# Gates and branches of a decoder's mixer by rows of tokens, the gates' first 512 columns as one seven-product unit, part of the weight splitting on GpSimd

## The chip, the core and the metric

The kernel runs on one core of a Trainium2 chip. The metric is the device time of one launch in microseconds. Before the change it is 1186.37 us, the median of three runs (1186.35 to 1187.4). The engines are called by their names in the profile: PE (TensorE, matmuls), PEld (its weight loads), DVE (VectorE), ACT (ScalarE), POOL (GpSimd), SP (SyncE, which issues most DMAs). Each of them works through its own queue in order.

## What is computed

A decoder trunk of two layers on 256 tokens of width 1024, all in float32. A layer is a feed-forward half step, a mixer, and another feed-forward half step. The change is in the mixer, which is this (shortened):

```python
z = x @ w_in
u, v, q, k, val, gates = jnp.split(z, SPLITS, axis=-1)
h_a = _chunked_sgu(gelu(u), gelu(v), sgu_ln_g, sgu_ln_b, sgu_w, sgu_b)
o = _diff_attention(_rope(q), _rope(k), val, lam_full)       # 8 heads, causal
h_b = _rmsnorm(o, diff_ln_g) * (1.0 - lam_init)
g = jax.nn.sigmoid(gates.reshape(bsz, seq, N_BRANCH, D_MODEL) + gate_b)
m = g[:, :, 0] * (h_a @ w_branch[0]) + g[:, :, 1] * (h_b @ w_branch[1])
return m @ w_out
```

Each of the seven parts of `w_in` (u, v, q, k, val, gate A, gate B), each branch matrix and `w_out` is 1024 x 1024.

## The kernel before

**Exactness.** A float32 product is made of three fast matmuls. Every operand is split into a high part (ScalarE copies it into the rounded format) and a low part (VectorE subtracts the high part from the value): hi and lo. A product is hi x hi, lo x hi and hi x lo. `split` (L245), `stream` (L176) and `pieces` (L362) do this.

**Weights** come in chunks of 128 x 2048 words (1 MB), loaded by SyncE into one of `RAW` = 4 buffers (`fetch`, L159). A chunk is two half chunks of 128 x 1024; for each, ScalarE writes a hi and VectorE a lo buffer, of which there are `HL` = 8 each. So weights are prepared up to four chunks ahead, and then the preparing engines wait until TensorE has given buffers back.

**Two forms of a projection.** By rows (`gemm_b`, L324, with `rows_b`, L314): 128 tokens of x are the stationary operand, 512 columns of weights stream by, the result stands tokens by columns. One step (128 of the inner dimension, 128 tokens) is three matmuls of 512 (L283). By columns (`gemm_a2`, L285): 128 columns of weights are stationary, and the hi and lo of x, 2 x 256 tokens, stream by as one matmul of 512 (L295), and for the lo weights hi of x alone, a matmul of 256 (L302). The result stands columns by tokens; it lies in two halves of a PSUM bank, so ScalarE copies one out (L303) and VectorE adds the other (L305).

**Seven products.** The feed-forward layers do part of their products by Strassen's scheme: 2 x 2 blocks (two blocks of 128 tokens by two of 512 inner dimensions, times two by two blocks of weights) take seven block products instead of eight. VectorE adds the blocks of x (`strassen_sums`, L860) and of weights (`plus`, L356), or a DMA on GpSimd's queue adds one weight block to another in its buffer (`gather`, L350). `product` (L372) is one of them: 12 matmuls of 512 (L376). They are taken one at a time between chunks of other work.

**Order.** TensorE's order is the program's. Work of the other engines that goes on beside it is written as generators with delays (`beside`, L137, `beat`, L124), counted in units of matmul work; two chunk halves by rows for both token blocks are two units. The order on the other engines is made by the scheduling layer from these priorities.

**The mixer (L969).** val by rows; then for each of four head pairs q and k by columns with rotary (`rope`, L984: the swapped copy goes by DMA, GpSimd multiplies it, L993), and `attend` (L1003) beside it: scores on TensorE (L1017), mask and maximum on VectorE (L1029), exponentials on ScalarE (L1031), differences on VectorE (L1040), a transpose by DMA that needs the 16-bit words of each number apart and joined again (`parted` by GpSimd L216, `joined` by ScalarE L1065), the product with val (L1071, L1073), then the root of the sum of squares as a chain of small operations on GpSimd (`rsqrt4`, L265 to L277), which ScalarE's scaling (L1090) waits for, and another transpose. The two gates follow, for each the first 512 columns by rows (`gate_rows`, L1119) and the second 512 by columns (`gate_columns`, L1130). Then u, v, spatial gating, and the branches: `branch_rows` (L1211) and `branch_columns` (L1243). The merged m is needed columns by tokens for the output projection; the half by rows is transposed (`turned`, L1222: L216 and L1227 part the words, SyncE's DMA transposes, L229 joins them), the half by columns is split at once. The output projection (`gemm_b2`, L467) takes m's first half of columns first for the first 128 tokens, and the second half first for the second.

Of the kernel before, what the change touches and what calls it, by code (L numbers as in the profile page):

```python
# [45 lines left out]
RAW, HL = 4, 8  # L46
RSQRT_START = -554050368.0

# [6 lines left out]
def trunk(ctx, tc, x, xT, w13a, w13b, w2, wb, wqk, wu, wg, wgr, wbr, wbrr, wo, gateb, gatebr, sgug, sgub, sguwT, sgubias, lam, diffg,  # L55
# [42 lines left out]
    def t512(s, n=3):  # L98
        return tmp.tile([P, 512], F32, tag="main", name=name(s), bufs=n)

    def s512(s, n=4):
        return tmp.tile([P, 512], F32, tag="side", name=name(s), bufs=n)
# [45 lines left out]
    line = [None, None, False]  # L148

# [26 lines left out]
    def stream(src, width=CH, sub=HC, lent=(), after=(None, None), pool=()):  # L176
# [3 lines left out]
        raw = fetch(src, width)  # L180
        out = []
# [174 lines left out]
    def plus(raw, more):  # L356
        for v, m in zip(halved(raw), halved(more)):
            with behind(line[1]):
                inline(V, V.tensor_tensor(out=v, in0=v, in1=m, op=ALU.add).ins)  # L359
        return raw  # L360

    def pieces(raw):  # L362
        out = []
        for v in halved(raw):
# [187 lines left out]
    gbh = const.tile([P, DEPTH, 2, KT], F32, name="gbh")  # L552
# [4 lines left out]
    def setup(after):  # L557
# [3 lines left out]
        for dst, src in ((x_tok[0], x[:P, :]), (x_tok[1], x[P:, :]), (cos_t, cosT), (sin_t, sinT), (dgs, diffg),  # L561
                         (gbh, gateb), (ln_g, lngT), (ln_b, lnbT), (lam_t, lam.partition_broadcast(P))):
# [6 lines left out]
        with behind(added[0]):  # L569
            V.tensor_scalar(out=gbh, in0=gbh, scalar1=0.5, scalar2=None, op0=ALU.mult)  # L570
# [23 lines left out]
    class Norm:  # L594
# [36 lines left out]
        def kept(self):  # L631

            y = self.y[-1][:, D - self.group :]
            unit, v = (tmp.tile([P, 512], F32R, tag="main", name=name("kept"), bufs=3) for _ in range(2))
# [145 lines left out]

    def ffn(l, f, i, norm, last=False):
# [57 lines left out]
        def sums_of_h():  # L839
# [3 lines left out]
            made.append([tmp.tile([P, 512], F32R, tag="side", name=name("sum"), bufs=4) for _ in range(2)])  # L843
            yield from strassen_sums(sums, made, h11, h21, h12, h22, 1.5)

        def sums_of_x():
# [6 lines left out]
            def home(tag):  # L853
                pool, n = {"main": (tmp, 3), "side": (tmp, 4), "slot": (act, 26)}[tag]
                return pool.tile([P, 512], F32R, tag=tag, name=name("xhs"), bufs=n)
# [3 lines left out]

        def strassen_sums(to, made, v11, v21, v12, v22, apart=1, after=lambda: None):  # L860
            to[:] = [tuple(lambda k, v=v: v[:, k * P : (k + 1) * P] for v in m) for m in made]
            for n, (out, a, b, op) in ((0, (v22, v21, v22, ALU.subtract)), (2, (v21, v11, v21, ALU.subtract)),
                                       (1, (v11, v22, v11, ALU.subtract)), (3, (v12, v12, v11, ALU.add))):
                with behind(after()):
                    V.tensor_tensor(out=out, in0=a, in1=b, op=op)
                if n in (2, 3):
                    yield apart
            for n, out in ((0, v22), (2, v21), (1, v11), (3, v12)):
                split(*(v if len(out.shape) == 2 else v.rearrange("p (k t) -> p k t", k=4) for v in made[n]), out)
                yield apart  # L870
# [98 lines left out]
    def mixer(l, i, norm):  # L969
        xh, xl = parts(both)  # L970
# [32 lines left out]
        def attend(hp, qT, kT):  # L1003
# [17 lines left out]
            def exps(t, banks):  # L1021
                nk = (t + 1) * P
                pp = []
                for m in range(2):
                    o = m * 4 + t * 2
                    p = s512("pp", 4)[:, : 2 * nk]
# [39 lines left out]
            yield 2 if hp else 1.5  # L1066
# [15 lines left out]
            yield 0.8  # L1082
# [3 lines left out]
            yield 3.6 if hp < 3 else 2.6  # L1086
# [4 lines left out]
            yield 0.4  # L1091
            onT = slots("onT", 2)[0]
            parted(on, onT)
            yield 3.4 if hp < 2 else 1.4
            moved(onT, on)
            yield 1.8
            with behind(added[0]):
                joined(on, onT, V)
            yield 0.3
# [9 lines left out]

        for hp in range(HEADS // 2):  # L1110
# [3 lines left out]
            if hp == 1:  # L1114
                gbias = bc_load(gatebr[l], qT[:, :1])

        gates, grow = [], []

        def gate_rows(br):  # L1119

            gr = [slots("gr", 2)[0] for _ in range(NT)]
            grow.append(gr)

            def done(t, ps, c, n):
                added[0] = V.tensor_tensor(out=gr[t], in0=ps, in1=gbias[:, br * 512 : (br + 1) * 512], op=ALU.add).ins
                emptied[0] = A.activation(gr[t], gr[t], AF.Tanh, scale=0.5).ins

            gemm_b(wgr[l, br, 0], KT, xh, xl, done, tail=TAIL)

        def gate_columns(br):  # L1130
            gt = slots("gate", KT // 2)
            gates.append(gt)
            for c in range(KT // 4):
                (_, b), = gemm_a2([wg[l, br, c]], both, lambda m: t512("gz"), lambda: t512("r"))
                for n in range(2):
                    s, k = slice(n * T, (n + 1) * T), KT // 2 + c * 2 + n
                    A.activation(gt[c][:, s], b[:, s], AF.Tanh, scale=0.5, bias=gbh[:, l, br, k : k + 1])

        for br in range(2):
            gate_rows(br)  # L1140
            gate_columns(br)

        g_bc, b_bc = (bc_load(v[l], gates[0][0][:, :1]) for v in (sgug, sgub))
# [214 lines left out]
```

## Time and profile before

| | us |
|---|---|
| median of three runs | 1186.37 (1186.35 to 1187.4) |
| span of the profiled execution, first to last instruction | 1185.1 |
| what lies around the span, median less span | 1.3 |
| PE busy | 1180.5 |
| DVE busy | 1013.1 |
| ACT busy | 828.1 |
| POOL busy | 287.5 |
| mean granted clock of TensorE | 1.000 |
| HBM read | 248.05 MB, 210 GB/s over the span |

How it is read: the page gives busy time and the chain of waits that ended last; groups give the mean time of an instruction by line and shape; the timeline gives start and length of instructions in order; windows give busy times by stretch. Busy rows of matmuls overlap, so what a matmul costs is read from the start of one to the start of the next. The first mixer stands at about 180 to 420 us, the second at about 770 to 1010.

### The profile page before, as it was taken

The numbers are of one execution on the slowest core, as the hardware profiler recorded it, in microseconds if no ns is written. First come the engines' busy times: TensorE is split into PE (matmuls) and PEld (weight loads), VectorE is DVE, ScalarE is ACT, GpSimd is POOL, SyncE is SP. The second block draws the span as 40 slices with busy tenths as digits, with TensorE's granted clock in tenths as the row PEclk, the third lists the DMA queues.
The fourth block names the chain that finished last, engine by engine and source line by source line (L and its number), as shares of the span: only waits on it lengthen the run. The fifth ranks groups of instructions, "written<-read, shape, count | busy, mean of one in ns | idle before, by whom it ended". The sixth has DMA issues, their size and how long they took to land.

```text
span 1185.1 us, 16676 instructions
## 1 busy us (share of the span) xinstructions
PE 1180.5 (100%) x5777; PEld 995.0 (84%) x5777; DVE 1013.1 (85%) x1562; ACT 828.1 (70%) x1419; POOL 287.5 (24%) x350
## 2 busy tenths in 40 slices
PE   9999999999999999999999999999999999999998
PEld 8888888888888888888888888888888888888887
DVE  6989989788688989889899889888965989988895
ACT  6688658559955677876667876576788556679761
POOL 1011201247420220051020161003564112102600
PEclk9999999999999999999999999999999999999999
DMA  9869976767865658699668689586666755786881
GB/s 355 265 198 262 287 273 208 266 193 238 246 205 173 227 188 273 187 275 267 239 220 265 190 278 280 198 290 232 212 204 208 250 181 174 247 254 208 273 260 36
DMA packets 129621, 275.10 MB, mean 232 GB/s; under 512 B 89041, under 2 KB 90369, under 8 KB 105473
## 3 DMA queue, kind: packets, MB, share of 16 engines
q1 hardware_dynamic: 121968, 248.67, 63.5%
q0 software_dynamic: 6992, 24.71, 8.7%
q8 instruction: 45, 0.74, 0.2%
q10 hardware_dynamic: 576, 0.66, 0.2%
q14 instruction: 40, 0.32, 0.1%
HBM read 248.05 MB, written 1.05 MB: 210 GB/s over the span
## 4 chain that ended last, share of the span: by engine, by line
PE 99%; DVE 0%; DVEq 0%; issue 0%
PE bank L283 46%; PE bank L295 15%; PE sbank L376 12%; PE bank L410 10%; PE bank L302 8%; PE sbank L410 3%; PE bank L530 2%; PE sbank L1017 1%; PE bank L376 1%; PE sbank L1073 1%; PE sbank L1191 1%; PE sbank L542 0%; PE sbank L1071 0%; PE sbank L714 0%; DVE xtok L701 0%; DVE st L643 0%
## 5 line engine op out<-in xcount | busy, mean ns | idle before, releaser
L197 DVE TENSOR_TENSOR wlo<-raw,whi 128x1024 fp32r<-128x1024 f32 (+1 forms) x346 | 379.4, 1123 | 51.8 <-ACT whi L195 38.0
L195 ACT ACTIVATE whi<-raw 128x1024 fp32r<-128x1024 f32 (+1 forms) x350 | 323.4, 952 | 135.1 <-PE bank L283 43.0
L283 PE MATMUL bank<-whi,x 128*128 128x512 f32 x1224 | 386.4, 390 | 0.0
L283 PEld LDWEIGHTS bank<-whi,x 128*128 128x128 f32 x1224 | 229.8, 188 | 47.8
L283 PE MATMUL bank<-wlo,x 128*128 128x512 f32 x612 | 238.2, 389 | 0.0
L249 DVE TENSOR_TENSOR wlo<-raw,whi 128x1024 fp32r<-128x1024 f32 (+1 forms) x123 | 142.9, 1185 | 20.3 <-ACT whi L247 11.4
L247 ACT ACTIVATE whi<-raw 128x1024 fp32r<-128x1024 f32 (+1 forms) x123 | 121.1, 1003 | 51.2 <-DVE raw L359 23.9
L295 PE MATMUL bank<-x,whi 128*128 128x512 f32 x640 | 153.3, 391 | 0.0
L295 PEld LDWEIGHTS bank<-x,whi 128*128 128x128 f32 x640 | 118.2, 188 | 23.8
L283 PEld LDWEIGHTS bank<-wlo,x 128*128 128x128 f32 x612 | 114.9, 188 | 23.1
L229 POOL COPY seven<-seven 128x512 uint16<-128x512 uint16 x16 | 58.8, 3733 | 135.2 <-ACT whi L195 54.6
L302 PEld LDWEIGHTS bank<-x,wlo 128*128 128x128 f32 x640 | 81.4, 191 | 2.9
L302 PE MATMUL bank<-x,wlo 128*128 128x256 f32 x640 | 82.6, 283 | 0.0
L410 PE MATMUL bank<-whi,hhi 128*128 128x512 f32 (+1 forms) x182 | 68.2, 374 | 0.0
L410 PE MATMUL bank<-whi,hlo 128*128 128x512 f32 (+1 forms) x182 | 67.9, 373 | 0.0
L410 PE MATMUL bank<-wlo,hhi 128*128 128x512 f32 (+1 forms) x182 | 67.9, 373 | 0.0
L993 POOL TENSOR_TENSOR swap<-swap,sin_t 128x512 f32<-128x512 f32 x16 | 26.9, 1680 | 101.2 <-DMA swap<-z 84.4
L757 POOL COPY nvia<-ntwo 128x256 uint16<-128x256 uint16 x20 | 10.0, 547 | 161.2 <-DMA ntwo<-nvia 148.2
L303 ACT ACTIVATE r<-bank 128x256 f32<-128x256 f32 x96 | 34.9, 373 | 16.3 <-PE bank L302 16.1
L376 PE MATMUL sbank<-whi,xhs 128*128 128x512 f32 x128 | 42.0, 389 | 0.0
L410 PEld LDWEIGHTS bank<-whi,hlo 128*128 128x128 f32 x182 | 34.3, 188 | 6.0
L410 PEld LDWEIGHTS bank<-whi,hhi 128*128 128x128 f32 x182 | 34.3, 188 | 6.0
(292 smaller groups left out, 2157.6 us busy)
## 6 DMA issues: line engine op xcount, KB each, us to landing
raw<-in_w13b SPq DMA_DIRECT2D x68, 1024.0 KB, 6.0
raw<-in_w SPq DMA_DIRECT2D x32, 1024.0 KB, 7.0
raw<-in_wb SPq DMA_DIRECT2D x16, 1024.0 KB, 6.7
raw<-in_wqk SPq DMA_DIRECT2D x16, 1024.0 KB, 6.2
home<-in_w13b SPq DMA_DIRECT2D x16, 512.0 KB, 5.9
raw<-in_w13a SPq DMA_DIRECT2D x8, 1024.0 KB, 4.9
home<-in_w SPq DMA_DIRECT2D x16, 512.0 KB, 4.9
raw<-in_wgr SPq DMA_DIRECT2D x8, 1024.0 KB, 5.4
```

The lines of the kernel that those rows point to most:

```text
L195: inline(A, A.activation(h, r, AF.Copy).ins)
L197: low = eng.tensor_tensor(out=w, in0=r, in1=h.bitcast(F32), op=ALU.subtract).ins
L229: eng.tensor_copy(out=o, in_=i)
L247: a = A.activation(hi, src, AF.Copy).ins
L249: return a, eng.tensor_tensor(out=lo, in0=src, in1=hi.bitcast(F32), op=ALU.subtract).ins
L283: PE.matmul(ps, xx, w, start=start and n == 0, stop=stop and n == 2)
L295: PE.matmul(b[-1], hi[:, k * P : (k + 1) * P], xc(k), start=k == 0, stop=False)
L302: PE.matmul(b[n][:, :T], lo[:, k * P : (k + 1) * P], xc(k)[:, :T], start=False, stop=k == KT - 1)
L303: emptied[0] = A.activation(r[:, s], b[n][:, T:], AF.Copy, scale=scale).ins
L376: PE.matmul(ps, x[o](k), y, start=start and k == n == 0, stop=stop and k == 3 and n == 2, skip_group_check=True)
L410: PE.matmul(q[c][t][:, :n] if o == 0 else more[:, :n], x(k, t), y, start=k == 8 and m == 0 and (c, t) != (1, 0) and not o, stop=k == FT - ...
L993: turned_by[0] = G.tensor_tensor(out=s3, in0=s3, in1=s, op=ALU.mult).ins
```

## The change

What it does, part by part:

1. The gates' first 512 columns (both gates, all 1024 of the inner dimension, 256 tokens) become one unit of seven products (`gates_by_rows`), with four sums of x blocks (`sums_of_x`, started 4 units into the rotary projections). The products are taken one each after the last chunk of the new `gate_rows` for gate A, after both chunks for gate B, after each of the first two u chunks, and after each half of v (`tick` 10 to 16). r1 is the buffer that holds the upper left weight block and the sums made in it; for product 2 GpSimd makes the sum and both lo parts, for products 3 and 5 VectorE sums, and r1 gets the lower left block added by DMA after product 3.
2. The gates' second 512 columns and the branches' second 512 go by rows, as their first halves do. The second half of m is now transposed too (`turned` with `half` = 1).
3. 13 half chunks in each mixer have their lo part made by GpSimd: four of the seven-product unit, and nine by `HELPED`, which counts the chunks of `stream` in the mixer: 1 to 4 val, 5 to 12 q and k of the head pairs in turn, 13 and 14 gate A, 15 and 16 gate B, 17 and 18 u, 19 to 22 v, 23 and 24 u, 25 to 32 branches, 33 to 36 output.
4. `RAW` is 5 instead of 4, the pools of work tiles have 4 and 6 instead of 3 and 4, and the room for descriptors of GpSimd's DMAs is 2048 bytes of a partition. Delays in `attend` and between later steps are set anew. `strassen_sums` moves out of `ffn`, unchanged.

The core of the diff:

```diff
-RAW, HL = 4, 8
+RAW, HL = 5, 8
+MAIN, SIDE = 4, 6
...
+HELPED = {10: (0,), 11: (1,), 13: (1,), 14: (1,), 19: (0,), 20: (1,), 26: (1,), 28: (0,), 30: (1,)}
...
         raw = fetch(src, width)
+        turn_of[0] += 1
+        pool = pool or HELPED.get(turn_of[0], ())
...
-    def plus(raw, more):
+    def plus(raw, more, eng=V):
         for v, m in zip(halved(raw), halved(more)):
-            with behind(line[1]):
-                inline(V, V.tensor_tensor(out=v, in0=v, in1=m, op=ALU.add).ins)
+            with behind(line[1] if eng is V else None):
+                a = eng.tensor_tensor(out=v, in0=v, in1=m, op=ALU.add).ins
...
-            for eng, ins in zip((A, V), split(hi, lo, v, after=line[:2])):
-                inline(eng, ins)
+            for eng, ins in zip((A, V), split(hi, lo, v, G if n in pool else V, after=(line[0], None if n in pool else line[1]))):
+                if n not in pool or eng is A:
+                    inline(eng, ins)
...
+            bx, r1 = bank(), fetch(w11)
+            product(bx, x11, pieces(r1, (0,)), True, False)
+            sum_up(g00, bx, bias[0], ALU.add)
+            yield
+            bz, r2 = bank(), fetch(w12)
+            product(bz, x_sums[0], pieces(plus(r1, r2, G), (0, 1)), True, False)
+            sum_up(g11, bz, bias[1], ALU.add)
+            yield
+            r3 = fetch(w22, raw=homes(lo_pool, "lo"))
+            product(bx, x_sums[1], pieces(plus(r1, r3)), False, False)
+            gather(r1, w21)
+            sum_up(g01, bias[1], bx, ALU.subtract)
+            yield
+            product(bz, x_sums[3], pieces(r3), False, True)
+            sum_up(g01, bz, g01, ALU.add, True)
+            yield
+            product(bx, x_sums[2], pieces(plus(r2, r3)), False, False)
+            sum_up(g11, g11, bx, ALU.subtract, True)
+            yield
+            product(bx, x22, pieces(r1), False, True)
+            sum_up(g10, bx, bias[0], ALU.add, True)
+            yield
+            bq = bank()
+            product(bq, x12, pieces(fetch(w21), (1,)), True, True)
+            sum_up(g00, bq, g00, ALU.add, True)
+            yield
...
+            if ticks[0] in (10, 11, 12, 13, 14, 15, 16):
+                next(products)
+
+        beside(sums_of_x(), 4.0)
...
-            beside(attend(hp, qT, kT), 4.5 + 2.1 * hp)
...
+            beside(attend(hp, qT, kT), (4.2, 5.0, 9.7, 10.0)[hp])
...
-            gemm_b(wgr[l, br, 0], KT, xh, xl, done, tail=TAIL)
-
-        def gate_columns(br):
...
+            ps = [bank() for _ in range(NT)]
+            for c in range(2):
+                for j, piece in enumerate(stream(wgr[l, br, half][:, c * CH : (c + 1) * CH])):
+                    for t in range(NT):
+                        rows_b(ps[t], t, 4 * c + 2 * j, piece, xh, xl, KT)
+                        if c and j:
+                            done(t, ps[t], 0, 512)
+                tick()
 
         for br in range(2):
-            gate_rows(br)
-            gate_columns(br)
...
+            gate_rows(1, br)
...
-        branch_rows(1, hb)
-        for _ in branch_columns(1, hb, ((0, 1),)):
-            pass
+        for half in range(2):
+            branch_rows(1, half, hb)
         m_hi += slots("mhi", KT, F32R)
         m_lo += slots("mlo", KT, F32R)
-        branch_rows(0, ha)
-        for c, m in branch_columns(0, ha, ((0,), (1,))):
-            V.tensor_tensor(out=m, in0=m, in1=gates[1][c], op=ALU.add)
-            settled = split(m_hi[KT // 4 + c], m_lo[KT // 4 + c], m, after=turned_rows)
+        for half in range(2):
+            branch_rows(0, half, ha)
```

How the order moves, at two places. The first is GpSimd's queue in the first mixer, from the rotary product of the last head pair's queries to the start of the first head pair's root chain. `swap` is the rotary product, `aT` and `d` the attention's copies, `wlo` a lo part, `raw` a weight buffer, `ss` the sum of squares. Before:

```order
L993 TENSOR_TENSOR swap_2384<-swap_2384,sin_t 128x512
L993 TENSOR_TENSOR swap_2486<-swap_2486,sin_t 128x512
L216 COPY aT_2481<-d_2479 128x512 x2
L216 COPY d_2480<-d_2480 128x256 x2
L1084 TENSOR_TENSOR ss_2578<-s_495_2579,ss_2578 128x4
L268 TENSOR_SCALAR ve_2617<-ss_2578 128x4
```

The same stretch after the change, beginning with product 1's lo part:

```order
L254 TENSOR_TENSOR wlo_2622<-raw_2619,whi_2621 128x1024
L364 TENSOR_TENSOR raw_2619<-raw_2619,raw_2744 128x1024 x2
L999 TENSOR_TENSOR swap_2439<-swap_2439,sin_t 128x512
L254 TENSOR_TENSOR wlo_2749<-raw_2619,whi_2748 128x1024
L999 TENSOR_TENSOR swap_2505<-swap_2505,sin_t 128x512
L221 COPY aT_2468<-d_2466 128x512 x2
L221 COPY d_2467<-d_2467 128x256 x2
L254 TENSOR_TENSOR wlo_2753<-raw_2619,whi_2752 128x1024
L1090 TENSOR_TENSOR ss_2597<-s_504_2598,ss_2597 128x4
L273 TENSOR_SCALAR ve_2663<-ss_2597 128x4
```

Three lo parts of 1024 columns and two sums of weights now stand among the attention's operations, one of the lo parts between the second head pair's copies and the first pair's root chain.

The second place is SyncE's queue at the end of the branches. `gr` is a half of m by rows, `in_wo` the output projection's weights, `in_w13b` those of the next feed-forward layer. Before:

```order
L173 DMA raw_4145<-in_wo 128x2048
L220 DMA_TRANSPOSE gr_2492<-gr_2773 128x8x128
L173 DMA raw_4310<-in_w13b 128x2048
L173 DMA raw_4340<-in_w13b 128x2048
L220 DMA_TRANSPOSE gr_2493<-gr_2774 128x8x128
L173 DMA raw_4384<-in_w13b 128x2048
```

After:

```order
L176 DMA raw_4247<-in_w13b 128x2048
L225 DMA_TRANSPOSE gr_2614<-gr_2616 128x8x128
L176 DMA raw_4277<-in_w13b 128x2048
L176 DMA raw_4321<-in_w13b 128x2048
L225 DMA_TRANSPOSE gr_2615<-gr_2617 128x8x128
L225 DMA_TRANSPOSE gr_2511<-gr_2642 128x8x128
L176 DMA raw_4351<-in_w13b 128x2048
L225 DMA_TRANSPOSE gr_2512<-gr_2643 128x8x128
```

Two transposes more stand there, those of the second half, each with a load of the next layer's weights ahead of it or near it.

More of the change, by code (lines that the diff above doesn't have):

```diff
@@ L633, in kept @@
             y = self.y[-1][:, D - self.group :]
-            unit, v = (tmp.tile([P, 512], F32R, tag="main", name=name("kept"), bufs=3) for _ in range(2))
+            unit, v = (t512("kept", F32R) for _ in range(2))
             self.unit, hi, lo = unit[:, :P], v[:, : self.group], v[:, self.group :]
@@ L779, in close, with strassen_sums @@
             return self
+    def strassen_sums(to, made, v11, v21, v12, v22, apart=1, after=lambda: None):
+        to[:] = [tuple(lambda k, v=v: v[:, k * P : (k + 1) * P] for v in m) for m in made]
+        for n, (out, a, b, op) in ((0, (v22, v21, v22, ALU.subtract)), (2, (v21, v11, v21, ALU.subtract)),
+                                   (1, (v11, v22, v11, ALU.subtract)), (3, (v12, v12, v11, ALU.add))):
+            with behind(after()):
+                V.tensor_tensor(out=out, in0=a, in1=b, op=op)
+            if n in (2, 3):
+                yield apart
+        for n, out in ((0, v22), (2, v21), (1, v11), (3, v12)):
+            split(*(v if len(out.shape) == 2 else v.rearrange("p (k t) -> p k t", k=4) for v in made[n]), out)
+            yield apart
     def ffn(l, f, i, norm, last=False):
@@ L842, in sums_of_h @@
             made = [[h_hi[1], h_lo[1]]] + [[slots("sum", 2, F32R)[0] for _ in range(2)] for _ in range(2)]
-            made.append([tmp.tile([P, 512], F32R, tag="side", name=name("sum"), bufs=4) for _ in range(2)])
+            made.append([s512("sum", F32R) for _ in range(2)])
             yield from strassen_sums(sums, made, h11, h21, h12, h22, 1.5)
@@ L858, in sums_of_x @@
             yield from strassen_sums(x_sums, made, t11, t21, t12, t22, after=lambda: None if norm else line[1])
[L860 to L870, printed above, removed]
         def seven(src, x_sums):
@@ L1108, in attend, with sums_of_x, gates_by_rows, sum_up @@
                                             op1=ALU.subtract)
+        x_sums = []
+        def sums_of_x():
+            made = [slots("xhs", 4, F32R) for _ in range(4)]
+            t11, t12, t21, t22 = (norm.rows[v] for v in ((0, 0), (0, 1), (1, 0), (1, 1)))
+            yield from strassen_sums(x_sums, made, t11, t21, t12, t22, 1.1, lambda: added[0])
+        grow = [[None] * 2 for _ in range(2)]
+        def gates_by_rows():
+            x11, x12, x22 = (tuple(lambda k, o=o, t=t, h=h: x_cat[h][:, k, o + t * P : o + (t + 1) * P] for o in (0, T))
+                             for t, h in ((0, 0), (0, 1), (1, 1)))
+            (w11, w21), (w12, w22) = ([wgr[l, br, 0][:, o : o + CH] for o in (0, CH)] for br in range(2))
+            for br in range(2):
+                grow[br][0] = [slots("gr", 2)[0] for _ in range(NT)]
+            (g00, g10), (g01, g11) = (grow[br][0] for br in range(2))
+            bias = [gbias[0][:, br * 512 : (br + 1) * 512] for br in range(2)]
+            def sum_up(out, in0, in1, op, end=False):
+                added[0] = V.tensor_tensor(out=out, in0=in0, in1=in1, op=op).ins
+                if end:
+                    emptied[0] = A.activation(out, out, AF.Tanh, scale=0.5).ins
+            bx, r1 = bank(), fetch(w11)
[24 more added lines that the diff above has]
+            yield
```

148 lines of the change are left out of this document (75 added, 73 removed).

## The prediction

> **What bounds the kernel now.** I read the page first: who is busy, at what clock, and what the chain of waits is made of.
>
> ```profile
> span 1185.1 us, 16676 instructions
> ...
> PE 1180.5 (100%) x5777; PEld 995.0 (84%) x5777; DVE 1013.1 (85%) x1562; ACT 828.1 (70%) x1419; POOL 287.5 (24%) x350
> ...
> PEclk9999999999999999999999999999999999999999
> ...
> PE 99%; DVE 0%; DVEq 0%; issue 0%
> ```
>
> TensorE is busy throughout at full granted clock, and 99% of the chain of waits is TensorE following itself. Nothing else is ever late by more than a tenth of a microsecond or so. So a matmul taken out is worth its full spacing, and every new wait costs its full length. A busy matmul row overlaps its neighbour, so the price of a matmul is read from start to start. The timeline of TensorE, end of the v projection and two column pairs of u, in the first mixer (start, length):
>
> ```profile
> 321.54 0.62 PE L283 MATMUL bank<-whi,x 128*128 128x512 f32 x2
> ...
> 335.15 0.61 PE L283 MATMUL bank<-whi,x 128*128 128x512 f32 x2
> 336.06 3.79 PE L295 MATMUL bank<-x,whi 128*128 128x512 f32 x16
> 339.68 2.08 PE L302 MATMUL bank<-x,wlo 128*128 128x256 f32 x16
> 341.59 3.82 PE L295 MATMUL bank<-x,whi 128*128 128x512 f32 x16
> ```
>
> By rows, twenty steps of three matmuls lie between the first two rows: 13.61/60 = 0.2268 us for 512 columns. By columns, 16 of 512 take 3.62 us (0.226 each), but 16 of 256 take 1.91 us: 0.1194 each, where half of 0.2268 would be 0.1134.
>
> **TensorE.** In each layer seven products replace eight: 12 matmuls of 512 less. Four halves (the gates' and the branches' second 512 columns) go from 32 matmuls of 512 and 32 of 256 to 48 of 512. Together 52 more of 512 and 128 fewer of 256 in each layer: 52 x 0.2268 - 128 x 0.1194 = 11.79 - 15.28 = -3.49 us, of which Strassen is -2.72. Two layers: -7.0 us. The attention and spatial matmuls stay. A product's matmul (L376) lasts as long in the groups as one by rows (L283), so a product should keep that spacing:
>
> ```profile
> L283 PE MATMUL bank<-wlo,x 128*128 128x512 f32 x612 | 238.2, 389 | 0.0
> L376 PE MATMUL sbank<-wlo,x 128*128 128x512 f32 x48 | 18.7, 389 | 0.0
> ```
>
> **The other engines.** The rows that price them, from the groups by line and shape (the last two numbers before the second bar are the total and the mean ns of one):
>
> ```profile
> L197 DVE TENSOR_TENSOR wlo<-raw,whi 128x1024 fp32r<-128x1024 f32 x268 | 327.5, 1242 | 48.2 <-ACT whi L195 36.7 <-issue 5.9 <-ACT d L1081 3.3
> L195 ACT ACTIVATE whi<-raw 128x1024 fp32r<-128x1024 f32 x268 | 275.8, 1052 | 86.5 <-PE bank L295 30.8 <-PE bank L283 23.1 <-PE bank L410 8.6
> L359 DVE TENSOR_TENSOR raw<-raw,home 128x1024 f32<-128x1024 f32 x32 | 39.0, 1233 | 0.0
> L303 ACT ACTIVATE r<-bank 128x256 f32<-128x256 f32 x96 | 34.9, 373 | 16.3 <-PE bank L302 16.1
> L865 DVE TENSOR_TENSOR held<-held,held 128x512 f32<-128x512 f32 x16 | 10.9, 684 | 0.0
> L1137 ACT ACTIVATE gate<-gz,gbh 128x256 f32<-128x256 f32 x16 | 7.7, 506 | 0.3 <-DVE gz L305 0.3
> L305 DVE TENSOR_TENSOR gz<-bank,r 128x256 f32<-128x256 f32 x16 | 6.4, 419 | 1.8 <-ACT r L303 1.8
> L1125 DVE TENSOR_TENSOR gr<-bank,bc 128x512 f32<-128x512 f32 x8 | 5.5, 685 | 3.2 <-PE bank L283 3.2
> L1126 ACT ACTIVATE gr<-gr 128x512 f32<-128x512 f32 x8 | 5.0, 624 | 5.4 <-DVE gr L1125 5.4
> L197 POOL TENSOR_TENSOR wlo<-raw,whi 128x512 fp32r<-128x512 f32 x4 | 5.1, 1296 | 12.6 <-ACT whi L195 12.6
> ```
>
> VectorE, per layer: 14 half chunks of the unit instead of 8, 13 handed to GpSimd, so 7 lo parts fewer (-8.7); four sums of weights (+4.9); four sums of x and their four lo parts (+5.5); three more additions out of PSUM (+2.1); second halves by rows, about -0.6 in the gates and -3.6 in the branches. Sum -0.4: nothing. ScalarE: 6 hi parts (+6.3), hi parts of the sums (+2.5), the gates' evictions and tanh by columns against rows (4 x 0.373 + 4 x 0.506 - 2 x 0.624 = 2.27 for each half, -4.5), the branches' evictions (-3.0), copies around the two new transposes (about +3): +4. GpSimd has no row for 1024 columns. Its 512 took 1.30, so 1024 costs at most 2.6; I take 2.5, twice the row less one start. 13 lo parts and 2 sums: 37.5 us per layer. The lower left weights come twice, once added into r1 by two DMAs on GpSimd's queue, and the bias takes one load more: 1.5 MB per layer, on DMA engines that the windows below show 0.68 busy. Those two DMAs wait until VectorE has read r1 for product 3. Queued behind them are the third head pair's copies, whose matmul comes 18 us of TensorE later: hidden, unless GpSimd is late already. The room for GpSimd's DMA descriptors shrinks, and no row shows what that costs. The slowest such loads land after
>
> ```profile
> home<-in_w POOLq DMA_DIRECT2D x8, 512.0 KB, 9.7
> ```
>
> and if the two of r1 went one after the other, that were 19 us, while product 6 comes some 28 us of TensorE after product 3: I take nothing.
>
> All this is off the path while prepared weights stay ahead of TensorE. How much the cover bears, the windows show (busy time of PE, PEld, DVE, ACT, POOL; clock; DMA share): the first mixer, its attention and gates, and two stretches of feed-forward layers.
>
> ```profile
> 204.00:420.00 216.00, 216.00 (x1179) 185.68 (x1178) 177.35 (x351) 147.13 (x324) 76.79 (x116) 1.00 0.68 217
> 265.00:325.00 60.00, 60.00 (x346) 51.80 (x345) 44.74 (x95) 56.41 (x148) 35.65 (x69) 1.00 0.82 240
> 500.00:520.00 20.00, 20.00 (x90) 16.55 (x89) 20.00 (x22) 18.90 (x27) 11.25 (x3) 1.00 0.81 259
> ```
>
> At 500 VectorE is busy 20 of 20 us and ScalarE 18.9, under the same kind of seven-product unit, and TensorE doesn't stop. Saturated helpers alone do not stall it for 20 us.
>
> **Where the cover is thin.** GpSimd and VectorE hinder each other. Timeline of both in the second mixer:
>
> ```profile
> 810.14 1.30 POOL L993 TENSOR_TENSOR swap<-swap,sin_t 128x512 f32<-128x512 f32 x1 [5.15 <-DMA swap<-z]
> ...
> 810.20 2.32 DVE L197 TENSOR_TENSOR wlo<-raw,whi 128x1024 fp32r<-128x1024 f32 x1 [1.12 <-issue]
> ```
>
> ```profile
> 838.10 2.38 POOL L993 TENSOR_TENSOR swap<-swap,sin_t 128x512 f32<-128x512 f32 x1 [6.22 <-DVE mx L1029]
> ...
> 838.11 1.21 DVE L197 TENSOR_TENSOR wlo<-raw,whi 128x1024 fp32r<-128x1024 f32 x1
> ```
>
> Whoever came first kept its time (1.30 and 1.21), the other was later by about that (2.32 and 2.38). The Trainium skill, page "SBUF — State Buffer", section "Who interferes with whom", says so as a rule: a VectorE instruction with two SBUF inputs and a GpSimd instruction that reads SBUF exclude each other, whole instruction by whole instruction. These rows agree with it. By that rule moving lo parts to GpSimd frees no shared time but doubles it.
>
> I price it in the attention and gates of a layer. On GpSimd's queue, from the lo part of the second gate chunk to that of product 2's second half, stand 4 lo halves, 2 sums, 4 rotary products and two sets of attention copies. The copies undisturbed:
>
> ```profile
> 240.60 1.20 POOL L216 COPY d<-d 128x256 uint16<-128x256 uint16 x2
> 241.75 0.61 POOL L216 COPY aT<-d 128x512 uint16<-128x512 uint16 x1
> ```
>
> So 4 x 2.5 + 2 x 2.5 + 4 x 1.3 + 2 x 2.4 = 25.0 us. TensorE needs 33.8 us meanwhile, by the prices above (two rotary chunks of 5.53, three chunks by rows of 5.44, product 1, half of product 2, some 2.3 of attention). VectorE's own two-input work there is some 11 us (five lo parts, seven rotary operations of 512, one head pair's differences). Sum 36 of 34: over, if nothing overlaps. And more than product 2 hangs on it. Behind that last lo part GpSimd does the root chain of the first head pair, and ScalarE's scaling of its output waits for it, in ScalarE's queue ahead of the third pair's exponentials and product 3's hi parts:
>
> ```profile
> L275 POOL TENSOR_SCALAR nwa<-nwa 128x4 f32<-128x4 f32 x24 | 12.4, 515 | 2.1
> L274 POOL TENSOR_TENSOR nwa<-nwa,ve 128x4 f32<-128x4 f32 x24 | 8.1, 337 | 1.9
> L1031 ACT ACTIVATE pp<-pp,mx 128x256 f32<-128x256 f32 x32 | 15.9, 499 | 13.9 <-DVE mx L1029 13.9
> L1090 ACT ACTIVATE on<-on,nwy 128x128 f32<-128x128 f32 x32 | 10.8, 397 | 6.8 <-POOL nwy L276 6.8
> ```
>
> Three rounds of four small operations are about 5 us, scaling 1.4, exponentials 4.6, hi and lo of product 3 about 3.5: 14.5 us, while product 3 starts 8.3 us after product 2's second half. GpSimd's stretch can't start before TensorE gives back the buffers of the third rotary key chunk. Undisturbed: 25.0 + 14.5 = 39.5 against 33.8 + 8.3 = 42.1, so 2.6 us to spare. With all 11 us of VectorE in its way: 8.4 late. Bounds of this place: 0 to 8.4 us per layer; a gain is excluded, as TensorE has no idle time to give back. I take 1: VectorE waits for GpSimd's rotary products itself, reads PSUM in between, and lets GpSimd on meanwhile; a third of the 11 us in its way would make it 1.1 late.
>
> A second place: the output projection now follows a branch half by rows, which must be transposed first; by columns it needed none. Between the last matmul of a token block and its use lie 2 x 5.44 = 10.9 us. Two VectorE operations (0.68 + 0.68), a copy by GpSimd and one by ScalarE side by side (1.2), the transpose, two copies back (1.1), hi and lo (0.8):
>
> ```profile
> gr<-gr SPq DMA_TRANSPOSE x4, 4.5
> ...
> on<-onT SPq DMA_TRANSPOSE x8, 7.2
> ```
>
> With 4.5 us the chain is 9.0, 1.9 to spare; with 7.2 it is 11.7, 0.8 late. Bounds 0 to 0.8 per layer, I take none.
>
> **Sum.** 1185.1 - 7.0 + 2 x 1.0 = 1180.1 of span. The runs' median 1186.37 lies 1.3 above the profiled span: 1181.4 us. Without any stall 1179.4.
>
> **Rivals.** 0.2% of 1186.4, some 2.4 us, is about what a measurement here tells from no change.
>
> *Eaten up.* Both places stall by 2.3 to 4.7 us per layer: 1184.0 to 1188.7, about 1186.4 at 3.5. For it: the 36 of 34. Against it: gap-free TensorE under full helpers at 500. Chance 0.14.
>
> *GpSimd becomes the bound (slower).* At the same place, if VectorE's instructions come back to back and keep GpSimd out, its queue falls behind by most of 11 us, product 3 waits through the root chain, and each queue is served in turn. That it can be kept out shows here, where two copies that take 0.9 to 1.2 each elsewhere lasted 10.5 under four lo parts of undisturbed pace:
>
> ```profile
> 503.39 10.51 POOL L229 COPY seven<-seven 128x512 uint16<-128x512 uint16 x2 [27.08 <-ACT whi L195]
> ```
> ```profile
> 506.90 4.63 DVE L197 TENSOR_TENSOR wlo<-raw,whi 128x1024 fp32r<-128x1024 f32 x4
> ```
>
> Price 8.4 and 0.8 per layer: 1179.4 + 2 x 9.2 = 1197.8; with two thirds of it 1191.7. It decides from 4.7 us per layer on. Against it: in the mixers VectorE is busy 177 of 216 us, not all, and part of that reads PSUM and stands in nobody's way. By the skill's rule above, taken strictly, this would be the likeliest case. Chance 0.24.
>
> *The change doesn't do what it says*, because the 256-column matmuls were no dearer than half of 512: then -5.4 instead of -7.0, 1183 us, still inside the forecast.
>
> **How the numbers follow.** Forecast (stall under 2.3 us per layer, 1179.4 to 1184.0): chance 0.62, with 1181.4 as its value. Range: down to 1179, the case without stall; up to 1196, which takes in "eaten up" and most of the slower case and leaves about 0.1 above. The forecast case's own range is 1179 to 1184. Faster by over 0.2%: 0.62; within: 0.14; slower: 0.24.
>
> **What would show it.** Right: 0.227 us per matmul in the products, PE 99% of the chain, no TensorE wait above 0.5 us in the gates. Wrong: a TensorE wait of microseconds at the lo parts of products 2 to 5, released by POOL or by VectorE and ScalarE behind it, with GpSimd's lo parts lasting well over 2.5 us; or a wait at the second half of the output projection's rows, released from the transposes.

## The result and the profile after

The changed kernel takes 1233.33 us (median of 5 runs, 1232.77 to 1235.35) against 1186.37 us before in the same job: 1.0399 times as long, 95% interval 1.0386 to 1.0411. 1181.4 us had been forecast, and 1196 was the upper end of the range. The page of the profiled execution after the change, its first lines and the engines' shares of the chain:

```profile
span 1232.9 us, 16431 instructions
...
PE 1190.8 (97%) x5625; PEld 990.2 (80%) x5625; DVE 1067.1 (87%) x1558; ACT 834.3 (68%) x1411; POOL 378.4 (31%) x393
...
PEclk9999999989999999999999999999999999999999
...
PE 68%; DVE 13%; POOL 6%; ACT 5%; issue 4%; DMA 3%; SPq 0%; DVEq 0%; ACTq 0%; POOLq 0%
```

TensorE carried 99% of the chain before and carries 68% now. VectorE is busy 54 us longer, although by the forecast's sum the change gives it no more work. TensorE is idle for 42.1 us of the span (1232.9 less 1190.8), before the change for 4.6. What TensorE waited for, in the trace after the change (released by which engine and line: us in all, times, longest):

```profile
PE bank L288 <- ACT vg L1223: 5.6, 2, 2.8
PE bank L288 <- DVE gr L1191: 4.8, 2, 2.8
PE sbank L1259 <- DVE vg L1238: 4.7, 2, 2.4
PE bank L300 <- DVE u L310: 4.2, 2, 2.8
PE bank L288 <- DVE z L312: 3.8, 2, 2.0
PE bank L300 <- DVE z L310: 2.9, 2, 2.6
PE bank L288 <- DVE x L254: 2.3, 2, 1.3
PE bank L300 <- DVE z L312: 2.2, 3, 1.0
PE sbank L1023 <- ACT on L1082: 1.6, 1, 1.6
PE bank L288 <- ACT mhi L1313: 1.4, 2, 1.1
PE sbank L719 <- DVE xtok L672: 1.2, 2, 0.6
```

All of these places lie in the two mixers and the projection and normalization that end them. Three things are to be seen. No row is released by GpSimd, nor by a lo part of weights. Most of the rows with `bank <-` an eviction (`u`, `z`, `gr`, and `vg` at L1223, ScalarE's Gelu) are waits for an output bank: the matmul has its operands and waits until VectorE or ScalarE has read the bank that it is to write. With 0.8 of u at L288, left out above, they make 24.3 us; `on` (1.6) is the same for a side bank, which ScalarE copies out (L1082). The others are operands: `vg` at L1238 (4.7 us) is v, normalized by VectorE, for the spatial product, and `x`, `mhi` and `xtok` (4.9 us) lie behind the transposes in front of the output projection.

The chain that ended last says which of these waits were paid for. From 238.0 to 375.5 us, in the first mixer, it holds no TensorE at all, and from 819.5 to 984.9 us in the second neither; it goes through the helpers. Some of its pieces in the first mixer (start, length; `wlo` is product 2's lo part by GpSimd, `on` L1096 the scaling behind the root chain, `pp` L1037 the exponentials, `d` the differences, `gr` L1191 the eviction of a gate):

```profile
275.84 2.37 POOL wlo L254
...
283.38 1.28 ACT on L1096 x4
284.67 1.04 ACT pp L1037 x5
...
290.78 1.26 DVE d L1046 x4
...
299.18 0.61 DVE gr L1191
...
374.77 0.75 DVE vg L1238
375.56 0.94 PE sbank L1259 x6
```

Between the first two rows stands the root chain; two more follow it (323 to 330 and 340 to 351 us), with GpSimd lo parts ahead of them (321.04 and 337.01). TensorE comes back at the spatial product, which waits 2.4 us for `vg`. By this chain, whose releasers are inferred, the bank waits before 375 us hold TensorE up early, and without them it would have waited for `vg` longer.

### The profile page after: what moved, and what is told of

It reads as the page before. It is cut to its first block, busy times and chain, and to the rows that moved or that the text cites. A ratio compares the mean times of both kernels' runs of the same rounds, so it can differ in the third digit from the quotient of the medians.

```text
span 1232.9 us, 16431 instructions
## 1 busy us (share of the span) xinstructions
PE 1190.8 (97%) x5625; PEld 990.2 (80%) x5625; DVE 1067.1 (87%) x1558; ACT 834.3 (68%) x1411; POOL 378.4 (31%) x393
## 4 chain that ended last, share of the span: by engine, by line
PE 68%; DVE 13%; POOL 6%; ACT 5%; issue 4%; DMA 3%; SPq 0%; DVEq 0%; ACTq 0%; POOLq 0%
PE bank L288 35%; PE sbank L384 11%; PE bank L418 9%; PE bank L300 4%; PE sbank L418 3%; DVE wlo L202 3%; PE bank L538 2%; PE bank L307 2%; DMA gr<-gr 2%; DVE d L1046 1%; ACT whi L200 1%; ACT pp L1037 1%; DMA on<-onT 1%; POOL wlo L254 1%; DVE qk L1003 1%
## 5 line engine op out<-in xcount | busy, mean ns | idle before, releaser
L288 PE MATMUL bank<-whi,x 128*128 128x512 f32 x1224 | 389.1, 391 | 14.2 <-ACT vg L1223 5.6
L200 ACT ACTIVATE whi<-raw 128x1024 fp32r<-128x1024 f32 (+1 forms) x334 | 305.0, 945 | 89.4 <-PE bank L418 31.4
L288 PEld LDWEIGHTS bank<-whi,x 128*128 128x128 f32 x1224 | 230.7, 188 | 64.6 <-ACT vg L1223 6.4
L288 PE MATMUL bank<-wlo,x 128*128 128x512 f32 x612 | 238.9, 390 | 0.0
L252 ACT ACTIVATE whi<-raw 128x1024 fp32r<-128x1024 f32 (+1 forms) x147 | 145.8, 1010 | 62.5 <-DVE raw L364 32.4
L300 PE MATMUL bank<-x,whi 128*128 128x512 f32 x512 | 126.0, 399 | 9.4 <-DVE u L310 4.2
L288 PEld LDWEIGHTS bank<-wlo,x 128*128 128x128 f32 x612 | 115.2, 188 | 23.5
L300 PEld LDWEIGHTS bank<-x,whi 128*128 128x128 f32 x512 | 96.7, 192 | 32.0 <-DVE u L310 5.1
L234 POOL COPY seven<-seven 128x512 uint16<-128x512 uint16 x16 | 67.1, 4252 | 128.1 <-DMA seven<-seven 86.2
L202 POOL TENSOR_TENSOR wlo<-raw,whi 128x1024 fp32r<-128x1024 f32 (+1 forms) x22 | 52.4, 2386 | 88.8 <-ACT whi L200 88.8
L307 PEld LDWEIGHTS bank<-x,wlo 128*128 128x128 f32 x512 | 64.9, 191 | 2.3
L307 PE MATMUL bank<-x,wlo 128*128 128x256 f32 x512 | 66.0, 283 | 0.0
L364 DVE TENSOR_TENSOR raw<-raw,home 128x1024 f32<-128x1024 f32 x40 | 48.6, 1229 | 0.8 <-DMA home<-in_w13b 0.8
L288 PE MATMUL bank<-whi,hb 128*128 128x512 f32 x128 | 43.1, 405 | 0.8 <-DVE u L310 0.8
L254 DVE TENSOR_TENSOR wlo<-home,whi 128x1024 fp32r<-128x1024 f32 x36 | 43.6, 1240 | 0.0
```

The source lines that it names most:

```text
L200: inline(A, A.activation(h, r, AF.Copy).ins)
L202: low = eng.tensor_tensor(out=w, in0=r, in1=h.bitcast(F32), op=ALU.subtract).ins
L234: eng.tensor_copy(out=o, in_=i)
L252: a = A.activation(hi, src, AF.Copy).ins
L254: return a, eng.tensor_tensor(out=lo, in0=src, in1=hi.bitcast(F32), op=ALU.subtract).ins
L288: PE.matmul(ps, xx, w, start=start and n == 0, stop=stop and n == 2)
```

## The experiments

All runs stand beside runs of the kernel before on the same chip, which gave medians of 1186.7 to 1187.1 us.

**All lo parts on VectorE** (1210.85 us, 1208.79 to 1216.19; 1.0212 of before, interval 1.0191 to 1.0233).

```
-HELPED = {10: (0,), 11: (1,), ...}
+HELPED = {}
-            product(bx, x11, pieces(r1, (0,)), True, False)
+            product(bx, x11, pieces(r1), True, False)
```

> The changed kernel with the thirteen lo parts and the two sums of weights of each mixer back on VectorE. Theory 'exclusion': a two-input instruction of VectorE and an instruction of GpSimd that reads SBUF don't run at once, so the 36 us of lo parts and sums on GpSimd in each mixer came off VectorE's time (its instructions lasted 41 us longer than undisturbed in the first mixer, 10 before the change). Then VectorE has 186 + 18 = 204 us of its own and some 10 of lengthening against 213 of TensorE: nearly all stalls go, 1180 to 1192, about 1186. Theory 'queue': GpSimd's small steps (rotary products, copies, roots) stood behind lo parts in its queue and came late, VectorE merely waited: then stalls go as well, and VectorE, no longer stretched, has 204 of 213: about 1180. Theory 'rows': the transposes and the sums of x that the change adds are what stalls, whoever makes lo parts: 1215 or more.

None of the three ranges holds it: 22.5 us of the loss go, 24 stay. The waits that stay, with 2.7 us in smaller rows at main banks (`gr` and `vg`) and 1.2 for `xtok`:

```profile
PE bank L300 <- DVE u L310: 5.3, 2, 2.8
PE bank L288 <- DVE z L312: 4.4, 3, 2.7
PE bank L288 <- DVE u L310: 2.7, 2, 2.6
PE bank L288 <- ACT mhi L1313: 2.5, 2, 1.4
PE bank L288 <- DVE x L254: 2.4, 2, 1.3
```

**Fills in place of GpSimd's pieces** (one run, 1208.96 us; these lo parts and sums are not computed).

```
+    def idle(like, out):
+        G.tensor_copy(out=out[:, :1], in_=like[:, :1])
+        for n in (HC, HC, HC // 2):
+            G.memset(out[:, :n].bitcast(F32), 0.0)
```

> The changed kernel, each lo part and sum of weights that GpSimd made in a mixer replaced, at the same place of its queue, by a one-column copy that waits for the same input and three fills of the buffer (2.5 times 1024 columns), which read no SBUF. These lo parts and sums are not computed. From the fills of 128 columns in the trace (0.2 us against 0.1 for one column) I estimate 2.4 us for the three, as long as a lo part. 'Exclusion': VectorE is not held up, its lengthening in a mixer falls from 41 to about 10 us and the stalls go: 1178 to 1184. 'Queue': the same steps stand behind the same length of work: 1222 to 1233. 'Rows': 1222 to 1233.

GpSimd is occupied as before, 2 x 0.958 + 0.524 = 2.44 us per piece beside the small copy:

```profile
L182 POOL MEMSET wlo<- 128x1024 f32 x52 | 49.8, 958 | 2.7
L182 POOL MEMSET wlo<- 128x512 f32 x26 | 13.6, 524 | 1.0
```

The first mixer's window (busy PE, PEld, DVE, ACT, POOL), up to about the same matmul, first of the changed kernel, then with fills:

```profile
204.00:447.00 243.00, 226.35 (x1129) 188.09 (x1128) 212.13 (x361) 152.57 (x322) 115.85 (x138) 0.98 0.66 199
```
```profile
204.00:435.00 231.00, 221.12 (x1122) 184.55 (x1121) 185.50 (x360) 153.05 (x321) 120.56 (x183) 0.99 0.67 208
```

VectorE runs the same instructions in 185.5 us instead of 212.1, while GpSimd is as busy. So GpSimd's reading, not its queue, cost VectorE 27 us in this mixer; "queue" falls as an account of that. But the time lies outside the range of "exclusion" too (1178 to 1184): 1209 us are as many as with all lo parts on VectorE, where VectorE has 18 us more of its own per mixer. That the rest of the loss hangs on neither is not shown by this: GpSimd, with the fills ahead of its root chains, has 8% of the chain that ended last here, and 3% with all lo parts on VectorE, where VectorE has 12% against 5%.

**Only the nine chunk halves back on VectorE** (`HELPED = {}` alone; 1220.91 us, 1220.49 to 1221.28).

> The changed kernel with the nine handed half chunks of each mixer back on VectorE, the unit's four lo parts and two sums still on GpSimd. All fifteen on GpSimd cost 22.5 us (1233.33 less 1210.85). 'Exclusion': the price goes by GpSimd's time, 6 of 15 pieces stay: 1210.85 + 9 = 1220, 1216 to 1224. 'Queue' by the unit alone (its pieces stand before the root chain): 1228 to 1233. 'Queue' by the handed chunks alone: 1209 to 1213.

"Exclusion" to within 1 us: 10 us for the six pieces per layer that stay, 12.4 for the nine that went.

**The kernel before, with nine lo parts handed over** (1194.36 us, 1193.04 to 1195.45; 1.0062, interval 1.0049 to 1.0076).

> The kernel before, with nine lo parts of each mixer (the same chunk numbers as in the change) made by GpSimd, nothing else changed. 'Exclusion': VectorE gives 9 x 1.2 = 11 us and is kept out for 9 x 2.4 = 22; its 196 busy us of 221 in the first mixer become about 207, which fits on the whole and not in the attention, where it was busy 53 of 61 us: 1188 to 1206, about 1195, and VectorE's instructions lengthened by 20 to 30 us per mixer. 'Queue': the rotary products behind the handed lo parts of the q and k chunks come late by up to 2.4 us each: 1186 to 1196, VectorE's instructions not lengthened. 'Rows': 1186, as before.

Handing over alone costs 7.2 us, which lies in the ranges of "exclusion" and of "queue". VectorE's time tells them apart: in the first mixer, up to about the same matmul, it is busy 185 us against 183 before (not 196, as the expectation has it), although nine lo parts, 11 us, are gone from it. So its instructions lasted some 13 us longer. TensorE waits in the attention only, for the evictions of q and k (4.7 us by the trace). The same nine cost 12.4 us in the changed kernel.

**The kernel before, with two main banks held** (1194.77 us, 1194.08 to 1195.23; 1.0067, interval 1.0052 to 1.0081).

```
+        def hold():
+            b = bank()
+            PE.matmul(b[:, :P], warm, warm, start=True, stop=True)
+            return lambda: PE.matmul(b[:, :P], warm, warm, start=True, stop=True)
```

> The kernel before, with two of its four main PSUM banks held idle over the stretch in which the unit holds its two: one from the end of the first gate to half of v, one from the rows of the second gate to the first u chunk. Two matmuls of 128 columns per bank hold it, 0.3 us in all. 'Banks': each chunk of that stretch waits for the eviction of the one before, some 1 to 2.5 us at five to six places per layer: 1193 to 1212, about 1200. 'VectorE is late' (and every other theory): 1186 to 1188.

7.9 us for nothing but two banks less; 5.0 of them are waits of the kind below, by the trace. The timeline at a gate's second chunk by columns shows how:

```profile
295.84 0.75 DVE L305 TENSOR_TENSOR gz<-bank,r 128x256 f32<-128x256 f32 x2
```
```profile
296.31 3.92 PE L295 MATMUL bank<-x,whi 128*128 128x512 f32 x16 [1.52 <-DVE gz L305]
```

The chunk needs two banks, two are held, two belong to the chunk before, whose last matmul ended at 294.8 and whose first sum VectorE finishes at 296.2. In the kernel before, two banks more cover that.

**Five main banks and three side banks**, all lo parts on VectorE (1224.37 us, 1224.16 to 1228.75).

> The run with all lo parts on VectorE (1210.85 us), with one of the eight PSUM banks moved from the side pool (attention, spatial) to the main pool: five main banks and three side ones instead of four and four. In that run's trace TensorE waited 15.1 us in all for evictions of main banks (u 5.3 and 2.7, z 4.4, the gates' sums 1.2 and 1.0, v 0.5). Theory 'banks': the unit holds one or two of four main banks from its first product to its sixth, so that a chunk by columns, which needs two, waits for the eviction of the chunk before; a fifth bank takes half to two thirds of those waits away: 1199 to 1204. Theory 'VectorE is late': the evictions are late because VectorE is, whatever the banks: 1208 to 1213. Three side banks may add waits at the attention's scores, which need four in turn, under either.

```profile
PE sbank L1023 <- DVE mx L1035: 17.8, 8, 3.5
PE sbank L1259 <- DVE vg L1238: 3.3, 2, 1.7
```

The time lies outside both ranges. The waits for evictions of main banks are gone, all 15.1 us, with VectorE as loaded as it was, and the attention pays for it: its scores take four side banks in turn and find three. Since TensorE is now held up for 17.8 us at the scores, most of it ahead of these evictions, VectorE also has more time for them. So this run doesn't show that the fifth bank alone took the waits away; what banks alone cost is shown by the previous run.

**Rows without unit and without GpSimd's pieces**, with delays in `attend` and behind it set for that (1202.81 us, 1198.04 to 1204.72; 1.0127, interval 1.0109 to 1.0144).

> The changed kernel without the Strassen unit and without handing over: both halves of gates and branches by rows, all lo parts by VectorE. TensorE has 1.5 us less in all than before the change, VectorE 4.2 us less per layer. 'Exclusion' and 'queue': no stall but up to 0.8 us per layer at the output projection's second half: 1184.8 to 1186.5. 'Rows': the two additional transposes stall the output projection by several us per layer: 1192 or more.

My "0 to 0.8 per layer" was too small, "rows" is right for this part. The waits, in the trace of its fastest run (1198.04 us):

```profile
PE sbank L1077 <- POOL aT L221: 4.5, 2, 3.4
PE bank L288 <- DVE x L254: 2.3, 2, 1.3
PE bank L288 <- ACT mhi L1308: 2.1, 2, 1.2
PE sbank L719 <- DVE xtok L672: 1.2, 2, 0.6
```

The first is the attention's copies by GpSimd: ahead of the longer wait two pairs of them lasted 2.80 and 2.26 us beside lo parts of VectorE, where a pair takes 1.20 undisturbed; the changed kernel has no such wait. The other three lie at the transposes. ScalarE, then VectorE there, second half of m:

```profile
402.48 0.78 ACT L1297 ACTIVATE gr<-gr 128x512 uint16<-128x512 uint16 x1 [4.18 <-DMA gr<-gr]
...
404.56 0.62 ACT L1288 ACTIVATE gr<-gr 128x512 uint16<-128x512 uint16 x1
...
408.39 0.80 ACT L1297 ACTIVATE gr<-gr 128x512 uint16<-128x512 uint16 x1 [1.35 <-DMA gr<-gr]
```
```profile
410.30 0.76 DVE L1310 TENSOR_TENSOR mlo<-gr,mhi 128x256 fp32r<-128x256 f32 x2
410.97 0.68 DVE L652 SCALAR_TENSOR_TENSOR xtok<-xtok,bank 128x512 f32<-128x512 f32 x1
```

The first block's words come back (402.48) 7.3 us after its transpose was issued. Behind that joining stands the second block's parting (404.56), ready since 400.4. So its transpose lands at 408.3, and its lo parts stand ahead of the sums (410.97) that the normalization needs.

**Parting ahead of joining**, with a later joining and otherwise the same (1195.01 us, 1194.25 to 1197.45).

```
+                first = (None, None) if t else parting[1]
+                with behind(first[0]):
                     A.activation(numbers(p)[:, 0], planes(g)[:, 0], AF.Copy)
```

> The run by rows without the unit (1202.81 us), with ScalarE's and GpSimd's parting of words for the second token block (second half of m) put ahead of the joining of the first block in their queues. In that run's trace the joining waited for its transpose and held the parting up from 399.7 to 404.6 us, the second transpose started 5 us late, its lo parts stood in VectorE's queue ahead of the output projection's sums, and the norm behind came late: TensorE waited 0.8 and 1.2 to 1.4 us per layer there, besides 1.1 to 1.3 us for the first block. Theory 'turned order': the two later waits go, 4.2 us in all: 1197 to 1200. Rival 'the transposes as such': the second transpose lands as late, or the waits move to the first block: 1201 to 1205.

7.8 us are won by the medians, more than the 4.2 of the waits; between the two traces it is 3.1 us of span (1196.1 to 1193.0). The waits for `xtok` and `x` are gone; those for `mhi`, the first block, stay at 1.5 us, and those for `aT` at 6.0.

**All three repairs together** (1203.93 us, 1202.64 to 1205.34), **the changed kernel with the banks' part alone** (1241.94 us, 1240.91 to 1247.9), **the kernel before with it** (1200.71 us, 1199.6 to 1201.37).

```
-            banks = [scores(t) for t in (1, 0)]
-            second, first = exps(1, banks[0]), exps(0, banks[1])
-            yield 1.2
+            second = exps(1, scores(1))
+            yield 0.7
+            first = exps(0, scores(0))
+            yield 0.8
```

> All lo parts on VectorE, five main and three side PSUM banks, the attention's scores of the first token block taken 0.7 units of matmul work after those of the second (so that three side banks do), and the turned order of parting and joining: the three causes that the runs point to, taken away together. From the run with all lo parts on VectorE (1210.85 us): less 15 us of waits for evictions, less some 3 us of lower clock after waits, less 4 us behind the transposes: 1188, 1184 to 1193. If the scores still wait as with three side banks before (17.8 us): 1206. If VectorE's load is a bound of its own (204 us undisturbed and 14 of lengthening against 213): 1193 to 1200.

> The changed kernel (GpSimd's fifteen pieces as they are) with five main and three side banks and the scores split as in the run beside. 'Exclusion' as a bound of its own: VectorE, held up by GpSimd, was busy 226 us of a mixer for which TensorE needs 213; without bank waits it must still stall by 13 us per layer, and 3 behind the transposes: 1207 to 1216. 'Exclusion' only through the banks: the 24 us of waits for evictions go and some 5 of clock: 1202 to 1206. 'Banks' don't matter once VectorE is this late: 1225 to 1233.

> The kernel before with the same bank split and split scores: what these two edits cost by themselves. TensorE never waits for a bank there: 1186 to 1188; if the later scores delay the attention: up to 1192.

The split of banks and scores is no neutral edit: in the kernel before it costs 14 us by itself, where at most 5 had been expected. 5.3 us of that are waits at the attention's product (L1072) by the trace; why the rest is lost was not followed. All three results lie outside every range given for them; the first is nearest to the 1206 for scores that still wait. So the first run shows that main banks and transposes no longer hold TensorE up much, and not that the repair is worth its price; its remaining waits are mostly banks that VectorE has to read, now the side ones (9.3 us). In the second run, 1242 is 26 us above the upper end by "exclusion". Its waits, beside 15.8 us at the scores:

```profile
PE sbank L1260 <- DVE vg L1239: 6.0, 2, 3.9
PE bank L288 <- DVE wlo L202: 5.0, 1, 5.0
PE sbank L1023 <- DVE qk L1003: 4.2, 2, 2.9
```

Here TensorE waits for VectorE's data too, a lo part for 5.0 us. Less the 14 us that the edit costs by itself, the time is some 5 us below that of the changed kernel, although 24.3 us of waits at main banks are gone. That fits the chain above, in which the helpers are the bound, with GpSimd in VectorE's way; it is no proof, as costs here don't simply add. No version that I ran beats the kernel before. Nor do the runs point to one: the unit saves 2.72 us of TensorE per layer, and six lo parts, four sums of weights, the sums of x and three additions cost VectorE or GpSimd some 20, by the forecast's own prices.

## Why the prediction was wrong

The step that failed is the stall term, 2 x 1.0 us. I took the mixers to be covered as the feed-forward stretch at 500 us is, where saturated helpers don't stall TensorE, and priced lateness at one place only, through lo parts, the root chain and the third head pair's exponentials to product 3. That path is there: it is the chain shown above, in both mixers. But no product waited for its lo parts. VectorE, which GpSimd's lo parts hold up, comes late to everything behind, and the helpers' chain is the bound for 137.5 us of the first mixer and 165.4 us of the second, with TensorE waiting at evictions and at last for `vg`. Of the two signs that I had named for being wrong, only the second came, the waits behind the transposes.

1. **TensorE, -7.0 us: right as a price.** Eleven spacings of product 2 take 2.49 us (281.85 to 284.34), 0.226 each, as by rows. Where the clock was lower a product took longer: product 3's matmuls follow each other at 0.426 us from 296.17 to 299.15.
2. **VectorE's net of -0.4 us per layer: right in instructions, wrong in time.** In the first mixer, up to about the same matmul, it was busy 212 us after the change and 183 before:

```profile
204.00:425.70 221.70, 221.70 (x1205) 190.40 (x1204) 182.84 (x365) 149.00 (x326) 76.79 (x116) 1.00 0.67 214
```

I priced the exclusion at one place, the gates, with 11 us of two-input work, and took 1 us per layer of bounds 0 to 8.4. GpSimd makes lo parts in the attention, v and the branches too. Two pairs from the trace after the change, GpSimd and VectorE:

```profile
237.81 2.46 POOL L202 TENSOR_TENSOR wlo<-raw,whi 128x1024 fp32r<-128x1024 f32 x1 [2.98 <-ACT whi L200]
...
240.59 2.47 POOL L202 TENSOR_TENSOR wlo<-raw,whi 128x1024 fp32r<-128x1024 f32 x1 [0.32 <-ACT whi L200]
```
```profile
238.58 1.71 DVE L1055 SCALAR_TENSOR_TENSOR c<-rc,neg_lam,sums 128x4 f32<-128x4 f32 x1
240.32 4.92 DVE L1046 SCALAR_TENSOR_TENSOR d<-pp,c,pp 128x256 f32<-128x256 f32 x4
```

An operation on four columns, 0.22 us otherwise, waits until GpSimd's lo part ends (237.81 + 2.46 = 240.27); the differences of one head pair, 1.41 us before, last 4.92 across the next. The price measured: 22.5 us for 30 pieces, 0.75 us each, where I had 2.0 us for all of them. The rival "GpSimd becomes the bound" had the right sign and the exclusion in it, but the other way round: it let VectorE keep GpSimd out, and counted 1197.8 from GpSimd's queue at one place. GpSimd's lo parts and sums lasted 2.64 us on average, not much over the 2.5 that I had taken; VectorE was kept out by them.

3. **PSUM banks: left out.** The rows of the trace before say `sbank<-` for a product (L376) and `bank<-` for a row matmul. The feed-forward unit accumulates mostly in side banks. In the mixer the attention has them, and the new code takes one or two of the four main ones from the first product to the last. Two banks less alone cost 7.9 us in the kernel before. No change of helpers' work is needed for that, so no sum over engines could find it. Where VectorE has all lo parts the waits at main banks come to 15.1 us, and what share of them the held banks have, and what share VectorE's lateness, is not shown.
4. **The transposes, 0 to 0.8 us per layer: the first block a little above its upper end, the second missed.** I wrote 11.7 us for the chain if a transpose takes 7.2; in the run by rows it took up to 7.3, and TensorE waited 1.2 and 0.9 us for the first block. I had not followed the second block: parting behind joining on ScalarE, lo parts ahead of the normalization on VectorE. Waits of 6.1 us in all with all lo parts on VectorE, and a gain of 3.1 us (traces) to 7.8 us (medians) when the order is turned in the run by rows.
5. **Late TensorE is also slow TensorE: left out.** The mean granted clock is 0.991. On 1232.9 us that is at most 11 us (last section).

The sum: 1186.4 - 7.0 + 22.5 (GpSimd's pieces, a difference of runs) + 15.1 (main banks) + 6.1 (transposes, both as waits in the trace with all lo parts on VectorE) = 1223.1. The 10 us missing to 1233.3 are missing in that run already: 1186.4 - 7.0 + 15.1 + 6.1 = 1200.6 against 1210.85. They are not idle time: TensorE was idle there for 26.0 us against 4.6 before, which these waits make up. It was busy 1183.1 us, where 1180.5 - 7.0 = 1173.5 had been forecast, and its clock of 0.996 accounts for at most 4.8 us of that. The rest is not settled. By steps between runs the loss of 46.2 us is 15.7 for the rows and transposes, 8.0 more for the unit with its banks and VectorE's work for it, and 22.5 more for GpSimd's pieces; the run by rows has delays and waits (`aT`) of its own, so the first two are rough. The parts also don't simply add: nine handed lo parts cost 7.2 us in the kernel before and 12.4 in the changed one.

## What to carry to other kernels

Before work is handed to GpSimd, reckon with up to its full time on VectorE wherever both read two operands from SBUF, and not with the difference of the two engines: here 15 pieces of 2.64 us lengthened VectorE's work in the first mixer by 27 us. When a unit is copied into another stage, count what it holds while it is interleaved, banks above all: a stage whose helpers are late by a microsecond or two runs without gaps only as long as its outputs have a bank to spare. Read the chain that ended last beside the list of waits: a wait of TensorE can cost nothing where a longer one stands behind it. And a chain through an in-order queue is followed for the second block too: what stands behind a wait is as late as the wait.

## What the runs showed of the hardware

A wait can cost more than its length. TensorE in the changed kernel, second mixer, and the window around it (the third figure from the end is the granted clock), then the one around another wait of the same length:

```profile
944.47 0.39 PE L288 MATMUL bank<-whi,x 128*128 128x512 f32 x1
947.65 0.60 PE L288 MATMUL bank<-whi,x 128*128 128x512 f32 x1 [2.79 <-ACT vg L1223]
948.05 0.63 PE L288 MATMUL bank<-wlo,x 128*128 128x512 f32 x1
948.48 1.05 PE L288 MATMUL bank<-whi,x 128*128 128x512 f32 x2
949.33 0.63 PE L288 MATMUL bank<-wlo,x 128*128 128x512 f32 x1
```
```profile
944.00:952.00 8.00, 5.21 (x16) 3.82 (x15) 8.00 (x7) 6.68 (x16) 5.67 (x5) 0.79 0.71 262
```
```profile
334.00:340.00 6.00, 3.23 (x15) 2.35 (x14) 6.00 (x5) 6.00 (x9) 2.99 (x1) 1.00 0.73 244
```

After the wait of 2.8 us the matmuls follow each other at 0.425 us (948.48 to 949.33 for two), not 0.227, for some 3.4 us. Not every wait of that length does it: around the one at 335 us the granted clock stays at 1.00. The Trainium skill, page "TensorE: Matmul & The Clock Gate", part 1 (the HAM clock gate), puts the half rate down to idleness in a free-running window of about 3.4 us; the rate agrees with these rows, and here a wait shorter than that window was enough.

GpSimd's fills did not hold VectorE up: its differences of 256 columns took 480 ns in that run, 483 before the change, and 874 with GpSimd's lo parts. The Trainium skill, page "SBUF — State Buffer", section "Who interferes with whom", says that a GpSimd instruction that only writes SBUF doesn't contend with VectorE's two-input instructions; this run agrees.
